# Hybrid decoder layer on one core: normalised x laid out at 2,304 bytes a part, input products cut at 256 columns, five offset places for split weights

## The chip, the core and the metric

The kernel runs on one core of one Trainium2 chip. The metric is device time in microseconds (us), from one launch of the program, lower is better. Five engines work side by side: PE (TensorE, matmuls; PEld is its weight load), DVE (VectorE), ACT (ScalarE), POOL (GpSimd) and SP (which here only issues DMAs). Each has its own in-order queue and waits for others by semaphores.

## What is computed

One decoder layer over 512 tokens of width 2,048 with 16 meta tokens put in front (528 columns in all), everything in float32:

```
n = rmsnorm(h) * g_mix;  p = n @ w_in           # 2048 x 6144
q, k, v, b, c, u = split(p, 6)                  # 1024 columns each
q, k = per-head rmsnorm (8 heads x 128)
z = q k^T / sqrt(128);  causal: key < query
w = exp(log_sigmoid(z) + reverse cumulative sum of log_sigmoid(-z))
o_attn = w v
o_conv = b * causal_conv3(c * u)
h = h + concat(rmsnorm(o_attn), rmsnorm(o_conv)) @ w_out
h = h + (silu(n2 @ w_gate) * (n2 @ w_up)) @ w_down;  n2 = rmsnorm(h)
return h without the meta columns
```

## The kernel before

All activations lie transposed: 128 channels on the partitions, tokens along the columns. Columns 0 to 15 are the meta tokens.

*Split products.* Matmuls run in the type float32r. To keep float32 accuracy each operand is split into a high part (the value cast to float32r) and a low part (value minus high part), and a product is the sum of three matmuls: high weights by high x (L168), high weights by low x (L170), low weights by high x (L172). ACT makes the high part by a cast, DVE the low part by a subtraction. Every matmul loads its 128 x 128 weights anew.

*Stage 1, start.* x arrives in 16 tiles xt (L233, SP's queue); split_x scales each by g_mix and makes nh and nl, two tiles of 528 columns (2,112 bytes a partition) for each of the 16; square_x gathers the squares for the norm. As the x tiles come in, the k and q products of head 0 run, FIRST giving the steps.

*Stage 1, weights.* prepare() loads weights into two places raw of eight 128-column tiles (512 KB a DMA, L132, SP), and splits four tiles at a time into whi (L136, ACT) and wlo (L137, DVE), each tag with five places; next_w keeps four sets ahead of the one in use. A set of a tag takes 2,048 bytes.

*Stage 1, products.* For each head k, q and v: k and v need all 528 columns, q needs 512. A PSUM bank holds 512 columns, so k and v go to two banks, 264 columns each. product_steps runs through the 16 x tiles, for each of them the matmuls of L168, L170 and L172 over all parts. Then qk_norm squares and copies the product out of PSUM (ACT), and after some tiles of the next product its finish normalises it (L328) and splits it for the attention; attend, sums and mix run in between the next products' matmuls, each released after a counted number of tiles by after and tick. After the eight heads come c, u and b for each of the eight channel groups: c and u in two halves of 258 columns (from column 12 on, since the convolution looks back two columns from column 16), b in 512.

*The rest.* The output projection (L670 to L672, weights w_out) and the feed-forward part (L684 to L686, a seven-product scheme in blocks of 256 columns) have their own pools of weights and activations. Their activations begin 16 bytes into a tile.

The steps of the prediction touch prepare (L126), product_steps (L161), split_x (L235), qk_norm (L302), head (L336), attend (L364) and the loop over c, u, b (L505 on), and the order of SP's DMA issues L132 and L233 at the start. The pieces that set the sizes:

```
H = L // 2
nh = npool.tile([P, L], F32R, tag=f"nh{k}", name=f"nh{k}")
product([(pv[:, 0, :H], 0, H), (pv[:, 1, :H], H, L)], n_hl)
C0, CH = 12, (L - 12) // 2
product([(pc[:, 0, :CH], C0, C0 + CH), (pc[:, 1, :CH], C0 + CH, L)], n_hl)
```

Of the kernel before, what the change touches and what calls it, by code (L numbers as in the profile page):

```python
# [9 lines left out]
F32 = mybir.dt.float32  # L10
# [5 lines left out]
P = 128  # L16
# [16 lines left out]
def hybrid_layer(ctx: ExitStack, tc: tile.TileContext, xT, w_in, w_out, w_gu, w_down, vecs, out):  # L33
# [47 lines left out]
        pe.matmul(warm[:, :P], ones, ones, start=True, stop=True)  # L81
    ident = const.tile([P, P], F32, name="ident")
    make_identity(nc, ident)
    later = const.tile([P, P], F32, name="later")
    gp.affine_select(
        out=later, in_=ones, pattern=[[-1, P]], compare_op=ALU.is_gt, fill=0.0, base=0,
        channel_multiplier=1,
# [31 lines left out]
                plan_w(w_in[c, b], 8)  # L119
    for b in range(2):  # L120
        plan_w(w_out[OUT_TILES[0], b], 8)
    raws, ready, taken = [], [], [0]
    SUB, AHEAD = 4, 4
    subs = [(i, a, min(a + SUB, n)) for i, (_, n) in enumerate(stream) for a in range(0, n, SUB)]

    def prepare():  # L126
        i, a, b = subs[len(ready)]
        with tc.high_priority():
            if i == len(raws):
                raws.append(wpool.tile([P, 8 * P], F32, tag="raw", bufs=2, name=f"raw{i}"))  # L130
                src, n = stream[i]
                nc.sync.dma_start(raws[i][:, : n * P], src)  # L132
            raw, c = raws[i][:, a * P : b * P], (b - a) * P
            hi = wpool.tile([P, SUB * P], F32R, tag="whi", bufs=AHEAD + 1, name=f"whi{i}_{a}")
            lo = wpool.tile([P, SUB * P], F32R, tag="wlo", bufs=AHEAD + 1, name=f"wlo{i}_{a}")
            sc.copy(hi[:, :c], raw)  # L136
            ve.tensor_tensor(lo[:, :c], raw, hi[:, :c].bitcast(F32), ALU.subtract)  # L137
        ready.append((hi, lo, b - a))
# [22 lines left out]
    def product_steps(parts, acts, n):  # L161

        k, last = 0, n - 1
        while k <= last:
            for wh, wl in next_w():
                ah, al = acts[k]
                for ps, a, b in parts:
                    pe.matmul(ps, wh, ah[:, a:b], start=k == 0, stop=False)  # L168
                for ps, a, b in parts:
                    pe.matmul(ps, wh, al[:, a:b], start=False, stop=False)  # L170
                for ps, a, b in parts:
                    pe.matmul(ps, wl, ah[:, a:b], start=False, stop=k == last)  # L172
                k += 1
                tick()
            yield
# [33 lines left out]

    H = L // 2  # L210
    n_hl = []
    accs = [rpool.tile([P, L], F32, name=f"acc_x{i}") for i in range(2)]

    acc = accs[0]
# [18 lines left out]
        nc.sync.dma_start(xts[k], xT[k])  # L233

    def split_x(k):  # L235
        nh = npool.tile([P, L], F32R, tag=f"nh{k}", name=f"nh{k}")
        nl = npool.tile([P, L], F32R, tag=f"nl{k}", name=f"nl{k}")
        g = g_mix[:, k : k + 1]
        if k < 4 or k % 2 == 0:
            sc.activation(nh, xts[k], AF.Copy, scale=g)  # L240
        else:
            gp.tensor_scalar(nh, xts[k], g, 0.0, ALU.mult, ALU.add)
        ve.scalar_tensor_tensor(nl, xts[k], g, nh.bitcast(F32), ALU.mult, ALU.subtract)
        n_hl.append((nh, nl))

    def square_x(k):
        if k < 2:
            sc.activation(accs[k], xts[k], AF.Square)
        else:
            s = t512(L, "r", 3)  # L250
            sc.activation(s, xts[k], AF.Square)
            (gp, ve)[k % 2].tensor_tensor(accs[k % 2], accs[k % 2], s, ALU.add)

    pk0 = pp.tile([P, 2, 512], F32, tag="pp", name="pk0")
    pq0 = pp.tile([P, 2, 512], F32, tag="pp", name="pq0")
    steps = [
        product_steps([(pk0[:, 0, :H], 0, H), (pk0[:, 1, :H], H, L)], n_hl, KT),
        product_steps([(pq0[:, 0, :], META, L)], n_hl, KT),
    ]
    prepare()  # L260
# [17 lines left out]


    apool = open_pool("apool", side="right")  # L280
    kns = [apool.tile([P, 640], F32, name=f"kn{i}") for i in range(1)]
    for t in kns:
        gp.memset(t[:, L:640], 0.0)
    oapool.tile([P, 8], F32, name="pad_oa")
    acc_c = oapool.tile([P, SEQ], F32, name="acc_c")
    acc_a = oapool.tile([P, SEQ], F32, name="acc_a")
# [6 lines left out]
    oa_all = o_slots(oapool, "oa", 4)  # L293
    oa = []

    def halves(ps, n):
        return ps[:, :, :n]

    def two(t):
        return t.rearrange("p (a b) -> p a b", a=2)  # L300

    def qk_norm(ps, g, cols, dst, parts_of, name):  # L302

        raw = t512(L, "e", 2)[:, :cols]
        s = t512(L, "e2", 2)[:, :cols]
        sh = apool.tile([P, L], F32R, tag="sh", name=f"sh_{name}")[:, :cols]
        sl = apool.tile([P, L], F32R, tag="sl", name=f"sl_{name}")[:, :cols]  # L310
        cuts = [(0, cols)] if cols == SEQ else [(0, H), (H, L)]
        raw_v, s_v = (raw, s) if cols == SEQ else (two(raw), two(s))
        sc.activation(s_v, ps, AF.Square)
        sc.activation(raw_v, ps, AF.Copy, scale=g)
        split(sh, sl, s)

        def finish():
            v = t512(L, "v", 2)[:, :cols]
            for a, b in cuts:
                q = small(f"ss_{name}{a}")[:, : b - a]  # L320
                pe.matmul(q, ones_r, sh[:, a:b], start=True, stop=False)
                pe.matmul(q, ones_r, sl[:, a:b], start=False, stop=True)
                ve.scalar_tensor_tensor(
                    v[:, a:b], q, 1.0 / P, eps_r2[:, L - cols + a : L - cols + b], ALU.mult, ALU.add
                )
            y = t512(L, "e2", 2)[:, :cols]
            rsqrt(y, v, cols)
            ve.tensor_tensor(dst, raw, y, ALU.mult)  # L328
            hi, lo, n = parts_of
            split(hi, lo, dst[:, :n])  # L330

        return finish

# [2 lines left out]
    def head(h):  # L336

        if h:
            pk = pp.tile([P, 2, 512], F32, tag="pp", name=f"pk{h}")
            product([(pk[:, 0, :H], 0, H), (pk[:, 1, :H], H, L)], n_hl)  # L340
        else:
            pk = pk0
        kn = kns[0]
        kh = apool.tile([P, 384], F32R, tag="kh", name=f"kh{h}")
        kl = apool.tile([P, 384], F32R, tag="kl", name=f"kl{h}")
        after(8, qk_norm(halves(pk, H), g_k, L, kn[:, :L], (kh, kl, 384), f"k{h}"))
# [6 lines left out]
        qn = apool.tile([P, SEQ], F32, tag="qn", name=f"qn{h}")  # L353
        qh = apool.tile([P, SEQ], F32R, tag="qh", name=f"qh{h}")
        ql = apool.tile([P, SEQ], F32R, tag="ql", name=f"ql{h}")
        after(9 if h else 10, qk_norm(pq[:, 0, :], gq_s, SEQ, qn, (qh, ql, SEQ), f"q{h}"))

        pv = pp.tile([P, 2, 512], F32, tag="pp", name=f"pv{h}")
        product([(pv[:, 0, :H], 0, H), (pv[:, 1, :H], H, L)], n_hl)
        vt = t512(L, "e", 2)  # L360
        ve.tensor_tensor(two(vt[:, :L]), halves(pv, H), two(r), ALU.mult)
        after(6 if h else 11, lambda: attend(h, kn, kh, kl, qn, qh, ql, vt))

    def attend(h, kn, kh, kl, qn, qh, ql, vt):  # L364
# [23 lines left out]
        pe.matmul(z[:, 272:416], kn[:, 384:512], qn[:, 368:], start=True, stop=True)  # L388
        pe.matmul(z[:, 416:432], kn[:, 512:640], qn[:, 496:], start=True, stop=True)


        lw = apool.tile([P, 1344], F32, tag="lw", name=f"lw{h}")
# [112 lines left out]
    C0, CH = 12, (L - 12) // 2  # L505
    oc = []
    for j in range(HEADS):
        pc = pp.tile([P, 2, 512], F32, tag="pp", name=f"pc{j}")
        product([(pc[:, 0, :CH], C0, C0 + CH), (pc[:, 1, :CH], C0 + CH, L)], n_hl)
        cu = t512(2 * CH, "e", 2)[:, : 2 * CH]  # L510
        ve.tensor_tensor(two(cu), halves(pc, CH), two(r2[:, C0:]), ALU.mult)
        pu = pp.tile([P, 2, 512], F32, tag="pp", name=f"pu{j}")
        product([(pu[:, 0, :CH], C0, C0 + CH), (pu[:, 1, :CH], C0 + CH, L)], n_hl)
        ve.tensor_tensor(two(cu), halves(pu, CH), two(cu), ALU.mult)
# [504 lines left out]
```

## Time and profile before

| | |
|---|---|
| three runs | 2108.03, 2109.98, 2113.12 us; median 2109.98 |
| profiled execution | 2107.92 us, of which the span from first to last instruction 2106.2 us |
| granted TensorE clock, mean | 0.998 of full speed |
| busy PE / DVE / ACT / POOL | 98 / 78 / 48 / 22% of the span |
| start, to the first pv matmul | 0 to 40.5 us |
| input products and attention | 40.5 to 627.5 us |
| output projection | about 627 to 775 us |
| feed-forward part | about 775 us to the end |

The page gives for each engine the busy time; a window row gives the same for a stretch of the execution. A row of the view in order of time reads: start, duration, engine, line, operation, out<-in, size, and in brackets what its engine waited for. Matmuls overlap in the pipeline, so what one costs is read from start to start. A row of a group reads: line, engine, operation, tiles, size, count, busy time and mean duration in ns of one, and then the idle time before them.

### The profile page before, as it was taken

What the parts mean: (1) busy time and instruction counts of PE and PEld (TensorE: products, weight loads), DVE (VectorE), ACT (ScalarE), POOL (GpSimd) and SP (SyncE); (2) the same over time, 40 slices, a digit from 0 to 9 for tenths busy, and PEclk for the clock granted to TensorE, in tenths of its full rate; (3) what the DMA queues carried; (4) which work ended last, traced back from release to release, by engine and by line L of the source; (5) the groups of instructions that cost most, each with busy time, mean ns of one, the idle gap of its engine ahead of it and who ended that gap; (6) DMA issues with size and microseconds to landing.
All of it is one profiled execution on the core that took longest, in us unless ns stands there. A gap on an engine that the chain in (4) does not pass through costs nothing.

```text
span 2106.2 us, 39382 instructions
## 1 busy us (share of the span) xinstructions
PE 2070.5 (98%) x16086; PEld 1987.5 (94%) x16086; DVE 1644.0 (78%) x2131; ACT 1019.5 (48%) x1576; POOL 458.9 (22%) x584
## 2 busy tenths in 40 slices
PE   8999999999999999999999999999999899999999
PEld 7999999999998888999999999999999899999999
DVE  8777767433337669999999998999989777877798
ACT  6666666322224344555555554555555444444443
POOL 4111111010003544122121221221111323122232
PEclk9999999999999999999999999999999999999999
DMA  5222222222235556566565565565554999788863
GB/s 173 81 72 80 74 78 81 81 97 94 91 110 172 177 181 221 166 184 179 172 190 166 154 193 165 172 178 160 170 153 146 304 280 278 202 232 246 241 190 121
DMA packets 146006, 342.48 MB, mean 163 GB/s; under 512 B 13393, under 2 KB 58961, under 8 KB 145825
## 3 DMA queue, kind: packets, MB, share of 16 engines
q1 hardware_dynamic: 67824, 214.33, 32.1%
q0 software_dynamic: 78000, 125.63, 21.9%
q8 instruction: 126, 2.06, 0.4%
q14 instruction: 56, 0.45, 0.1%
HBM read 268.60 MB, written 71.30 MB: 161 GB/s over the span
## 4 chain that ended last, share of the span: by engine, by line
PE 87%; DVE 5%; DMA 4%; issue 2%; ACT 1%; POOL 0%; SPq 0%; DVEq 0%; ACTq 0%
PE x L684 10%; PE x L686 9%; PE x L685 9%; PE z L684 5%; PE z L685 5%; PE z L686 5%; PE y L686 3%; PE y L685 3%; PE y L684 3%; PE po L671 3%; PE po L670 3%; PE po L672 3%; DMA b<-w_down 2%; DVE s L600 2%; PE pv L168 2%
## 5 line engine op out<-in xcount | busy, mean ns | idle before, releaser
L599 ACT CAST s<-t 128x1024 fp32r<-128x1024 f32 (+2 forms) x304 | 286.3, 942 | 395.3 <-PE z L686 127.6
L600 DVE TENSOR_TENSOR s<-t,s 128x1024 fp32r<-128x1024 f32 (+2 forms) x304 | 343.4, 1129 | 94.0 <-ACT s L599 92.5
L686 PE MATMUL x<-f,s 128*128 128x256 f32 x1408 | 387.3, 275 | 1.5 <-DVE s L600 1.5
L685 PE MATMUL x<-f,s 128*128 128x256 f32 x1408 | 387.4, 275 | 1.3 <-DVE f L183 1.3
L684 PE MATMUL x<-f,s 128*128 128x256 f32 x1408 | 387.3, 275 | 0.2 <-ACT f L182 0.2
L599 ACT CAST s<-b 128x1024 fp32r<-128x1024 f32 (+2 forms) x228 | 214.7, 942 | 221.7 <-PE x L686 202.1
L686 PEld LDWEIGHTS x<-f,s 128*128 128x128 f32 x1408 | 264.3, 188 | 1.7 <-DVE s L600 1.7
L685 PEld LDWEIGHTS x<-f,s 128*128 128x128 f32 x1408 | 264.3, 188 | 1.7 <-DVE f L183 1.5
L684 PEld LDWEIGHTS x<-f,s 128*128 128x128 f32 x1408 | 264.3, 188 | 0.5 <-ACT f L182 0.4
L600 DVE TENSOR_TENSOR s<-b,s 128x1024 fp32r<-128x1024 f32 (+2 forms) x228 | 248.1, 1088 | 3.1 <-ACT s L599 2.5
L137 DVE TENSOR_TENSOR wlo<-raw,whi 128x512 fp32r<-128x512 f32 (+1 forms) x198 | 142.3, 720 | 130.9 <-ACT whi L136 130.3
L868 POOL DMA_DIRECT2D fd<-s x154 | 108.8, 921 | 583.6 <-DVE s L183 582.1
L136 ACT CAST whi<-raw 128x512 fp32r<-128x512 f32 (+1 forms) x198 | 121.3, 614 | 185.3 <-PE pu L170 65.5
L684 PE MATMUL x<-ring,s 128*128 128x256 f32 x704 | 195.7, 278 | 8.6 <-DVE d L713 5.6
L684 PE MATMUL z<-f,s 128*128 128x256 f32 x704 | 195.8, 278 | 3.3 <-ACT p L705 3.1
L685 PE MATMUL x<-ring,s 128*128 128x256 f32 x704 | 194.8, 277 | 3.3 <-DMA ring<-fd 3.3
L686 PE MATMUL x<-ring,s 128*128 128x256 f32 x704 | 195.0, 277 | 0.4 <-DVE s L600 0.4
L686 PE MATMUL z<-f,s 128*128 128x256 f32 x704 | 193.9, 275 | 0.0
L685 PE MATMUL z<-f,s 128*128 128x256 f32 x704 | 193.9, 275 | 0.0
L606 DVE TENSOR_TENSOR t<-b,b 128x1024 f32<-128x1024 f32 (+2 forms) x152 | 166.4, 1094 | 27.8 <-DMA b<-w_down 23.2
L684 PEld LDWEIGHTS x<-ring,s 128*128 128x128 f32 x704 | 132.7, 189 | 10.7 <-issue 8.5
L684 PEld LDWEIGHTS z<-f,s 128*128 128x128 f32 x704 | 132.1, 188 | 6.5 <-ACT p L705 6.3
(326 smaller groups left out, 5599.0 us busy)
## 6 DMA issues: line engine op xcount, KB each, us to landing
b<-w_gu SPq DMA_DIRECT2D x176, 512.0 KB, 3.6
raw<-w_in SPq DMA_DIRECT2D x92, 512.0 KB, 3.3
fd<-s POOLq DMA_DIRECT2D x154, 256.0 KB, 5.3
b<-w_down SPq DMA_DIRECT2D x64, 384.0 KB, 3.9
ring<-fd POOLq DMA_DIRECT2D x28, 768.0 KB, 12.2
b<-w_down SPq DMA_DIRECT2D x64, 320.0 KB, 4.8
ring<-fd POOLq DMA_DIRECT2D x28, 640.0 KB, 11.3
wide<-w_out SPq DMA_DIRECT2D x30, 512.0 KB, 3.4
```

The lines of the kernel that those rows point to most:

```text
L136: sc.copy(hi[:, :c], raw)
L137: ve.tensor_tensor(lo[:, :c], raw, hi[:, :c].bitcast(F32), ALU.subtract)
L599: sc.copy(hi, src)
L600: ve.tensor_tensor(lo, src, hi.bitcast(F32), ALU.subtract)
L606: ve.tensor_tensor(sums[name], a, b, ALU.add)
L670: pe.matmul(ps, hi[:, kk], ah, start=k == 0, stop=False)
L671: pe.matmul(ps, hi[:, kk], al, start=False, stop=False)
L672: pe.matmul(ps, lo[:, kk], ah, start=False, stop=k == 7)
L684: pe.matmul(ps, hi[:, kk], act[:, 0, k], start=start and k == 0, stop=False, skip_group_check=not start)
L685: pe.matmul(ps, hi[:, kk], act[:, 1, k], start=False, stop=False, skip_group_check=not start)
L686: pe.matmul(ps, lo[:, kk], act[:, 0, k], start=False, stop=k == n - 1, skip_group_check=not start)
L868: gp.dma_start(fd[c][s][:, :, k], t[:, :, i])
```

## The change

- The normalised x is one tile n_all. Each of the 32 parts (high and low of 16 tiles) takes 576 columns, 2,304 bytes, which is nine times 256, and begins 4 columns in: all parts begin at the same residue modulo 256. In the layout of the program that is 240, the residue at which the feed-forward part's activations begin before and after.
- k, v, c and u go in parts of 256 and 272 columns: 256 into the second half of the first bank, 272 into the second bank, so that the 528 columns lie in one run in PSUM, and are read as one (across). c and u are now computed from column 0; the result is read from column 12 on as before.
- Split weights: high and low part lie in one tile w of 1,048 columns with five places. The part of it that is used begins at an offset that goes through 4, 0, 4, 8, 20 columns in turn. In the layout the five places begin at 16, 128, 48, 224 and 176 modulo 256; before, all began at 224.
- Raw weights: three places of four tiles, 256 KB a DMA, instead of two of eight.
- kn and qn keep only the columns that attend reads unsplit (144 of 528 and of 512; kn with its zeros is 256 wide), and the split parts are taken from the product in place; the mask "later" is a temporary.

On SP's queue the order of issues at the start becomes: three raw loads, xt 0 and 1, three raw loads, xt 2 to 4, three raw loads, xt 5 to 7, and so on; before: two raw loads, xt 0 to 2, two raw loads, xt 3 to 5, one raw load, xt 6, and so on.

```diff
-    later = const.tile([P, P], F32, name="later")
+    later = t512(P, "r", 3)
...
+    OFFSETS = (4, 0, 4, 8, 20)
...
-            if i == len(raws):
-                raws.append(wpool.tile([P, 8 * P], F32, tag="raw", bufs=2, name=f"raw{i}"))
-                src, n = stream[i]
-                nc.sync.dma_start(raws[i][:, : n * P], src)
-            raw, c = raws[i][:, a * P : b * P], (b - a) * P
-            hi = wpool.tile([P, SUB * P], F32R, tag="whi", bufs=AHEAD + 1, name=f"whi{i}_{a}")
-            lo = wpool.tile([P, SUB * P], F32R, tag="wlo", bufs=AHEAD + 1, name=f"wlo{i}_{a}")
+            c = (b - a) * P
+            raw = wpool.tile([P, SUB * P], F32, tag="raw", bufs=3, name=f"raw{i}_{a}")[:, :c]
+            nc.sync.dma_start(raw, stream[i][0][:, a * P : b * P])
+            at = OFFSETS[len(ready) % (AHEAD + 1)]
+            t = wpool.tile([P, 2 * SUB * P + 24], F32R, tag="w", bufs=AHEAD + 1, name=f"w{i}_{a}")
+            hi, lo = (t[:, at + h * SUB * P :][:, : SUB * P] for h in range(2))
...
+    LP = 576
+    n_all = npool.tile([P, 2 * KT * LP], F32R, name="n_all")
...
-        nh = npool.tile([P, L], F32R, tag=f"nh{k}", name=f"nh{k}")
-        nl = npool.tile([P, L], F32R, tag=f"nl{k}", name=f"nl{k}")
+        nh, nl = (n_all[:, a : a + L] for a in (4 + 2 * k * LP, 4 + (2 * k + 1) * LP))
...
+    def parts_of_two(ps, a, b):
+        return [(ps[:, 0, 512 - T2 :], a, a + T2), (ps[:, 1, : b - a - T2], a + T2, b)]
+
+    def across(ps, n):
+        return ps.rearrange("p a b -> p (a b)")[:, 512 - T2 : 512 - T2 + n]
...
-    kns = [apool.tile([P, 640], F32, name=f"kn{i}") for i in range(1)]
-    for t in kns:
-        gp.memset(t[:, L:640], 0.0)
+    kn = apool.tile([P, 256], F32, name="kn")
+    gp.memset(kn[:, L - 384 :], 0.0)
...
-        raw_v, s_v = (raw, s) if cols == SEQ else (two(raw), two(s))
-        sc.activation(s_v, ps, AF.Square)
-        sc.activation(raw_v, ps, AF.Copy, scale=g)
+        sc.activation(s, ps, AF.Square)
+        sc.activation(raw, ps, AF.Copy, scale=g)
...
-            ve.tensor_tensor(dst, raw, y, ALU.mult)
+            ve.tensor_tensor(dst, raw[:, late:], y[:, late:], ALU.mult)
             hi, lo, n = parts_of
-            split(hi, lo, dst[:, :n])
+            ve.tensor_tensor(raw[:, :n], raw[:, :n], y[:, :n], ALU.mult)
+            split(hi, lo, raw[:, :n])
...
-        product([(pv[:, 0, :H], 0, H), (pv[:, 1, :H], H, L)], n_hl)
+        product(parts_of_two(pv, 0, L), n_hl)
         vt = t512(L, "e", 2)
-        ve.tensor_tensor(two(vt[:, :L]), halves(pv, H), two(r), ALU.mult)
+        ve.tensor_tensor(vt[:, :L], across(pv, L), r, ALU.mult)
...
-        pe.matmul(z[:, 272:416], kn[:, 384:512], qn[:, 368:], start=True, stop=True)
-        pe.matmul(z[:, 416:432], kn[:, 512:640], qn[:, 496:], start=True, stop=True)
+        pe.matmul(z[:, 272:416], kn[:, :P], qn, start=True, stop=True)
+        pe.matmul(z[:, 416:432], kn[:, P:], qn[:, 128:], start=True, stop=True)
...
-        product([(pc[:, 0, :CH], C0, C0 + CH), (pc[:, 1, :CH], C0 + CH, L)], n_hl)
-        cu = t512(2 * CH, "e", 2)[:, : 2 * CH]
-        ve.tensor_tensor(two(cu), halves(pc, CH), two(r2[:, C0:]), ALU.mult)
+        product(parts_of_two(pc, 0, L), n_hl)
+        cu = t512(CN, "e", 2)[:, :CN]
+        ve.tensor_tensor(cu, across(pc, L)[:, C0:], r2[:, C0:], ALU.mult)
```

k's product (heads 0 to 7) and u's change as v's and c's do; the calls of qk_norm hand it the column from which the late part is kept, 384 for k and 368 for q.

More of the change, by code (lines that the diff above doesn't have):

```diff
@@ L121, in hybrid_layer @@
         plan_w(w_out[OUT_TILES[0], b], 8)
-    raws, ready, taken = [], [], [0]
+    ready, taken = [], [0]
+    OFFSETS = (4, 0, 4, 8, 20)
     SUB, AHEAD = 4, 4
@@ L256, in hybrid_layer @@
     steps = [
-        product_steps([(pk0[:, 0, :H], 0, H), (pk0[:, 1, :H], H, L)], n_hl, KT),
+        product_steps(parts_of_two(pk0, 0, L), n_hl, KT),
         product_steps([(pq0[:, 0, :], META, L)], n_hl, KT),
@@ L294, in hybrid_layer, with qk_norm @@
     oa = []
-    def halves(ps, n):
-        return ps[:, :, :n]
     def two(t):
         return t.rearrange("p (a b) -> p a b", a=2)
-    def qk_norm(ps, g, cols, dst, parts_of, name):
+    def qk_norm(ps, g, cols, late, dst, parts_of, name):
         raw = t512(L, "e", 2)[:, :cols]
@@ L339, in head @@
             pk = pp.tile([P, 2, 512], F32, tag="pp", name=f"pk{h}")
-            product([(pk[:, 0, :H], 0, H), (pk[:, 1, :H], H, L)], n_hl)
+            product(parts_of_two(pk, 0, L), n_hl)
         else:
             pk = pk0
-        kn = kns[0]
         kh = apool.tile([P, 384], F32R, tag="kh", name=f"kh{h}")
         kl = apool.tile([P, 384], F32R, tag="kl", name=f"kl{h}")
-        after(8, qk_norm(halves(pk, H), g_k, L, kn[:, :L], (kh, kl, 384), f"k{h}"))
+        after(8, qk_norm(across(pk, L), g_k, L, 384, kn[:, : L - 384], (kh, kl, 384), f"k{h}"))
         if h:
@@ L352, in head @@
             pq = pq0
-        qn = apool.tile([P, SEQ], F32, tag="qn", name=f"qn{h}")
+        qn = apool.tile([P, 144], F32, tag="qn", name=f"qn{h}")
         qh = apool.tile([P, SEQ], F32R, tag="qh", name=f"qh{h}")
         ql = apool.tile([P, SEQ], F32R, tag="ql", name=f"ql{h}")
-        after(9 if h else 10, qk_norm(pq[:, 0, :], gq_s, SEQ, qn, (qh, ql, SEQ), f"q{h}"))
+        after(9 if h else 10, qk_norm(pq[:, 0, :], gq_s, SEQ, 368, qn, (qh, ql, SEQ), f"q{h}"))
         pv = pp.tile([P, 2, 512], F32, tag="pp", name=f"pv{h}")
-        product([(pv[:, 0, :H], 0, H), (pv[:, 1, :H], H, L)], n_hl)
+        product(parts_of_two(pv, 0, L), n_hl)
         vt = t512(L, "e", 2)
-        ve.tensor_tensor(two(vt[:, :L]), halves(pv, H), two(r), ALU.mult)
+        ve.tensor_tensor(vt[:, :L], across(pv, L), r, ALU.mult)
         after(6 if h else 11, lambda: attend(h, kn, kh, kl, qn, qh, ql, vt))
@@ L503, in scale_a @@
         token_scale(acc_a, acc_a, 1024, "a", (sh, sl, t512(SEQ, "v", 2)[:, :SEQ], None, None))
-    C0, CH = 12, (L - 12) // 2
+    C0 = 12
+    CN = L - C0
     oc = []
@@ L508, in hybrid_layer @@
         pc = pp.tile([P, 2, 512], F32, tag="pp", name=f"pc{j}")
-        product([(pc[:, 0, :CH], C0, C0 + CH), (pc[:, 1, :CH], C0 + CH, L)], n_hl)
-        cu = t512(2 * CH, "e", 2)[:, : 2 * CH]
-        ve.tensor_tensor(two(cu), halves(pc, CH), two(r2[:, C0:]), ALU.mult)
+        product(parts_of_two(pc, 0, L), n_hl)
+        cu = t512(CN, "e", 2)[:, :CN]
+        ve.tensor_tensor(cu, across(pc, L)[:, C0:], r2[:, C0:], ALU.mult)
         pu = pp.tile([P, 2, 512], F32, tag="pp", name=f"pu{j}")
-        product([(pu[:, 0, :CH], C0, C0 + CH), (pu[:, 1, :CH], C0 + CH, L)], n_hl)
-        ve.tensor_tensor(two(cu), halves(pu, CH), two(cu), ALU.mult)
+        product(parts_of_two(pu, 0, L), n_hl)
+        ve.tensor_tensor(cu, across(pu, L)[:, C0:], cu, ALU.mult)
         y = t512(SEQ, "e2", 2)[:, :SEQ]
```

## The prediction

> **What bounds the kernel now.** I read the page first (busy shares, the chain of waits), then the stages by time window, then the instructions of TensorE in order of time, where the distance between two starts is the true price of a matmul; its own duration overlaps with the next one's and is of no use here.
>
> ```profile
> span 2106.2 us, 39382 instructions
> PE 2070.5 (98%) x16086; PEld 1987.5 (94%) x16086; DVE 1644.0 (78%) x2131; ACT 1019.5 (48%) x1576; POOL 458.9 (22%) x584
> PE 87%; DVE 5%; DMA 4%; issue 2%; ACT 1%; POOL 0%; SPq 0%; DVEq 0%; ACTq 0%
> 6.39:40.50 34.11, 28.95 (x148) 24.79 (x149) 32.94 (x39) 23.04 (x41) 20.70 (x14) 0.95 0.59 191
> 40.50:627.50 587.00, 585.97 (x4062) 549.47 (x4061) 351.30 (x604) 278.39 (x496) 68.19 (x126) 1.00 0.26 87
> ```
>
> The last two rows are windows: length, then busy time (and count) of PE, weight load, DVE, ACT and POOL, granted clock, DMA share, GB/s. The change touches two stages. From 6.39 to 40.5 us x arrives, is scaled and split, and heads 0 of k and q are multiplied; there VectorE is the full engine (32.94 of 34.11 us) and TensorE waits. From 40.5 to 627.5 us come all other input products and the attention; there TensorE is busy 585.97 of 587.00 us at clock 1.00, VectorE only 351. So in the second stage every nanosecond off a matmul is off the time; in the first none is.
>
> **What a matmul costs by its columns.** Starts in order of time (start, own duration, then the group):
>
> ```profile
> 1002.74 0.28 PE L686 MATMUL x<-f,s 128*128 128x256 f32 x1
> 1004.10 0.28 PE L686 MATMUL x<-f,s 128*128 128x256 f32 x1
> ...
> 207.07 0.40 PE L170 MATMUL pv<-nl,whi 128*128 128x264 f32 x2
> 209.72 0.40 PE L168 MATMUL pv<-nh,whi 128*128 128x264 f32 x2
> ...
> 479.14 0.40 PE L168 MATMUL pb<-nh,whi 128*128 128x512 f32 x1
> 490.24 0.40 PE L168 MATMUL pc<-nh,whi 128*128 128x258 f32 x2
> 501.81 0.40 PE L168 MATMUL pu<-nh,whi 128*128 128x258 f32 x2
> ...
> 768.04 0.39 PE L671 MATMUL po<-oc,s 128*128 128x512 f32 x1
> 769.40 0.39 PE L671 MATMUL po<-oc,s 128*128 128x512 f32 x1
> ```
>
> 256 columns: 12 matmuls in 1.36 us, 113.3 ns. 264 columns: 11 pairs in 2.65 us, 120.5 ns each. 258 columns: the whole product pc, 96 matmuls from 490.24 to 501.81, 120.5 ns each. 512 columns: 226.7 ns at best (6 in 1.36 us), 231.3 in pb (48 from 479.14 to 490.24). What the reader is to see: 258 and 264 cost the same, and 113.3, 120.5 and 226.7 are 16, 17 and 32 times 7.08 ns. The price goes by started groups of 16 columns, 7.08 ns each. Two halves of 264, or of 258, are 17 + 17 groups, 241.0 ns; 256 + 272 would be 16 + 17 groups, 233.7 ns. That is the core of the forecast.
>
> **The change part by part.** (a) *Parts of 256 and 272 for k, v, c, u.* A product is 16 tiles x 3 matmul pairs = 48 pairs:
>
> ```profile
> L168 PE MATMUL pv<-nh,whi 128*128 128x264 f32 x256 | 52.7, 287 | 0.0
> L168 PE MATMUL pc<-nh,whi 128*128 128x258 f32 x256 | 51.7, 284 | 0.0
> L168 PE MATMUL pb<-nh,whi 128*128 128x512 f32 x128 | 50.3, 393 | 0.0
> 144.07 0.28 PE L383 MATMUL z<-qh,kh 128*128 128x272 f32 x1
> 144.44 0.41 PE L388 MATMUL z<-qn,kn 128*128 128x144 f32 x2
> ```
>
> 256 rows of one kind over 8 heads are 16 pairs a product; three kinds make the 48. Without k's head 0, which lies in the first stage, 31 products remain in the saturated stage, 1488 pairs. At 233.7 for 241.0 ns that is 7.3 x 1488 = -10.9 us. Nothing here shows a 272 beside a 256. The nearest rows for 272 are the attention's three, 144.07 to 144.44: 123.3 ns each, 2.9 above 17 groups. With these the pair is 236.6 and the term -6.5 us. The other end is that both parts pay a group more than their number, as a part may that starts off its group: 247.9 ns, +10.3 us. I take -10.9, because the row with the same start (the x<-f rows of 256 columns begin, like all parts after the change, at 240 modulo 256 bytes in the layout) shows no excess in a thousand matmuls. That c and u now also multiply the 12 first columns, which nobody reads, is in the 233.7.
>
> (b) *Equal starts and the five places.* Before, the tiles of 2,112 bytes begin at four residues modulo 256; after, all parts begin at one, and the weights at five that depend on the place. For q and b (512 columns, 15 products x 48 = 720 matmuls in the stage) only this changes.
>
> ```profile
> 760.18 0.39 PE L670 MATMUL po<-oa,s 128*128 128x512 f32 x1
> 763.87 0.40 PE L671 MATMUL po<-oa,s 128*128 128x512 f32 x1
> 764.11 0.39 PE L672 MATMUL po<-oa,s 128*128 128x512 f32 x1
> 765.72 0.40 PE L670 MATMUL po<-oc,s 128*128 128x512 f32 x1
> ```
>
> Equal residues alone don't make 512 clean: oa has them too and averages 230.8 ns (24 in 5.54 us), a single one 240, while oc shows 226.7. From 231.3 the term lies between -3.3 us (226.7) and +6.3 us (240). I take 0: the nearest average, oa's, is where pb is already. The attention's operands also shift within their groups, some 35 matmuls a head; at half a group, 3.5 ns, that is +-1.0 us, taken as 0.
>
> (c) *Weights raw in three pieces of 4 tiles, not two of 8.* Twice as many DMA issues on SP.
>
> ```profile
> raw<-w_in SPq DMA_DIRECT2D x92, 512.0 KB, 3.3
> raw<-w_in SPq DMA_DIRECT2D x6, 256.0 KB, 2.8
>   DMA raw<-w_in: 3.5, 4
> ```
>
> A piece is reloaded when the piece three before has been split and is wanted three pieces later; four tiles are 12 pairs, 2.9 us, so it has 8.7 us for a landing of 2.8. The third row says what ACT waited for raw in the whole program: 3.5 us in 4 times. Nothing is behind these issues on SP in the saturated stage. Cost 0; without that cover every piece would be late by its landing less 2.9 us, which is below nothing.
>
> (d) *The start.* Here the moved issues count.
>
> ```profile
> 1.73 1.37 SPq L233 DMA_DIRECT2D xt<-xT  x3
> 5.49 0.81 SPq L132 DMA_DIRECT2D raw<-w_in  x2
> 6.34 1.37 SPq L233 DMA_DIRECT2D xt<-xT  x3
> 11.25 0.41 PE L168 MATMUL pk<-nh,whi 128*128 128x264 f32 x2
> 35.74 0.51 PE L170 MATMUL pk<-nl,whi 128*128 128x264 f32 x2 [1.43 <-DVE nl L243]
> ```
>
> SP issues x tiles 0 to 2 before its first wait now. After the change only tiles 0 and 1 stand there; tile 2 follows three raw loads, the last of which waits until VectorE has split the third piece, about 6.3 us by the start of the second raw pair here. So tile 2 is issued at about 6.7 instead of 3 us and lands near 10; on ACT its scaling stands behind the cast of the sixth piece, which waits for TensorE to be done with the first weights, near 10.7. TensorE wants tile 2 at 11.25 and gets it about 1 us late. The later x tiles move both ways, and VectorE, the full engine, has the same work in both. I take +1.0 us, between 0 (VectorE makes it up) and +3.
>
> (e) *The rest.* qk_norm multiplies the late 144 columns and the split columns apart: one more VectorE instruction.
>
> ```profile
> L328 DVE TENSOR_TENSOR kn<-tmp,tmp 128x528 f32<-128x528 f32 x8 | 5.6, 700 | 0.0
> L328 DVE TENSOR_TENSOR qn<-tmp,tmp 128x512 f32<-128x512 f32 x8 | 5.5, 686 | 0.1
> L183 DVE TENSOR_TENSOR kl<-kn,kh 128x384 fp32r<-128x384 f32 x8 | 4.4, 555 | 0.0
> 139.37 0.68 DVE L183 TENSOR_TENSOR ql<-qn,qh 128x512 fp32r<-128x512 f32 x1
> 143.07 0.39 PE L384 MATMUL z<-ql,kh 128*128 128x512 f32 x1
> ```
>
> By the slope from 384 to 528 columns (1.0 ns a column) 144 columns are 315 ns: k pays 315 + 555 - 700 = 170, q 315 ns, 0.49 us a head. ql is done at 140.05 and first used at 143.07: 3 us of cover, so 0; with no cover 8 x 0.49 = 3.9 us. Reading 516 or 528 columns in one run instead of two halves has the same count; the smaller kn, qn and the moved mask cost nothing.
>
> Sum: -10.9 + 0 + 0 + 1.0 + 0 = -9.9 us. The profiled execution took 2107.92 us (span 2106.2 and 1.7 around it), 0.1 below the lowest of the three runs and 2.1 below their median of 2109.98. From the profile the sum gives 2098.0, from the median 2100.1; I forecast 2099.0.
>
> **The rivals.** (1) *The 272 pays like the attention's*: the pair is 236.6, -6.5 + 1.0, 2103.5. For it: most matmuls in the trace whose columns are a whole number of groups lie above it (pb 231.3, oa 230.8). Against: x<-f. (2) *The excess eats the gain*: 256 and 272 have no slack inside their last group, where 258 and 264 hid misfits in 14 and 8 free columns; both pay half a group, 3.5 ns, the pair is 240.8, and the time 2109, no change. For it: pb and oa, half a group or more above 226.7. (3) *Slower: the price goes by columns, not by groups.* k and v keep their 528, c and u grow from 516 to 528 a pair; at (226.7 - 113.3) / 256 = 0.443 ns a column that is 5.3 ns x 768 pairs, +4.1, with the start 2114. It decides as soon as 258 is cheaper than 264; against it stand the rows, 120.5 for both. The Trainium skill has this rule: TensorE: Matmul & The Clock Gate, section Back-to-back issue gap, gives N / 2.4 + 2.5 ns on a warm clock, so 220.0 ns for 2 x 258 and 225.0 for 256 + 272, +3.8 us as an estimate from that page; the trace disagrees with it in level (113.3 where it has 109.2) and in the step from 258 to 264. (4) *Slower: both parts pay a whole group more*, since weights and x now meet in five fixed relations and a bad one repeats in every tile: 247.9 ns, +10.3 + 1.0, 2120. For it: 240 for a single oa matmul that recurs in each tile; against: x<-f and oc, with fixed relations and no excess.
>
> **How the numbers follow.** Forecast 0.55, rival 1 0.13, rival 2 0.11, rival 3 0.12, rival 4 0.09. 0.2%, some 4.2 us, is about what a measurement can tell from no change: faster is the forecast and rival 1, 0.68; the same is rival 2, 0.11; slower are rivals 3 and 4, 0.21. The likeliest case alone reaches from 2095 (512s clean as oc) to 2104 (start +3, attention +1). The range takes in rivals 1 to 3: 2093 to 2115; rival 4 is left out.
>
> **What would show it.** Right: in order of time, pairs of pv and pc 0.234 us apart, where 0.241 stands now; the window from the end of the start to the end of pb about 11 us shorter with TensorE still full; pb near 0.231; everything after it as long as before. Rival 1 shows 0.236 to 0.237, rival 2 0.241, rival 3 pc alone slower, rival 4 0.248. The start is wrong if the first pv begins before 40.5 or after 43.5 us. I'd be wrong altogether if TensorE begins to wait in the middle stage (for weights, or z for ql).

## The result: slower by 0.26%, and the profile after

The changed kernel took 2116.93 us in the median of ten runs (2112.93 to 2122.33), the kernel before 2113.12 us (2108.03 to 2119.12) beside it. The ratio is 1.0026, with a 95% interval of 1.0014 to 1.0039, some 3.0 to 8.2 us slower; the two medians by themselves lie 3.8 us apart. The forecast was 2099.0. The profiled execution took 2116.4 us, its span 2114.7 us, 8.5 more than before. That is more than the ratio gives: the profiled execution of before was faster than any of its ten runs.

The page of the changed kernel: the span, the busy times, the shares of the chain of waits, and the raw loads:

```profile
span 2114.7 us, 39641 instructions
PE 2076.6 (98%) x16086; PEld 1990.4 (94%) x16086; DVE 1652.8 (78%) x2147; ACT 1019.3 (48%) x1576; POOL 451.2 (21%) x584
PE 87%; DVE 6%; DMA 3%; issue 2%; ACT 2%; POOL 0%; SPq 0%; DVEq 0%; ACTq 0%; POOLq 0%
raw<-w_in SPq DMA_DIRECT2D x190, 256.0 KB, 2.8
```

Nothing new bounds it: TensorE is as full as before. So the windows are compared, cut at the same events in both kernels: the first matmul of head 0's v, of head 1's k, and of the last b, and for the third window the first matmul of x in the feed-forward part (columns as in the prediction's windows). Before:

```profile
6.39:40.52 34.13, 28.97 (x148) 24.81 (x149) 32.96 (x39) 23.06 (x41) 20.70 (x14) 0.95 0.59 191
54.54:616.15 561.61, 561.61 (x3911) 527.65 (x3909) 334.45 (x577) 268.10 (x479) 66.34 (x124) 1.00 0.26 83
807.05:2106.20 1299.15, 1271.38 (x11068) 1261.83 (x11066) 1133.82 (x1323) 644.32 (x924) 286.22 (x349) 1.00 0.67 195
```

After:

```profile
6.39:44.66 38.27, 30.90 (x149) 24.95 (x149) 33.26 (x40) 22.93 (x41) 17.91 (x14) 0.87 0.56 186
58.12:622.94 564.82, 564.67 (x3910) 529.47 (x3909) 343.79 (x593) 268.06 (x478) 61.47 (x124) 1.00 0.26 83
813.67:2114.70 1301.03, 1273.03 (x11068) 1263.04 (x11066) 1133.49 (x1323) 644.32 (x924) 286.05 (x349) 1.00 0.67 195
```

The reader is to see two places. The start is 4.1 us longer (38.27 for 34.13), though VectorE has the same work (33.26 and 32.96 us busy), and TensorE's granted clock is lower (0.87 for 0.95). The middle stage, where 11 us were to be gained, is 3.2 us longer (564.82 for 561.61), full in both, at full clock. The feed-forward part is 1.9 us longer, but that is not the change's: two executions of one kernel further down (two raw places) differ by 4.5 us in all that follows the middle stage, 1494.7 and 1490.2. The middle stage, however, repeats: 564.82 in both of these.

The price of a matmul in order of time, after:

```profile
485.37 0.39 PE L168 MATMUL pb<-n_all,w 128*128 128x512 f32 x1
496.51 0.41 PE L168 MATMUL pc<-n_all,w 128*128 128x256 f32 x2
508.14 0.40 PE L168 MATMUL pu<-n_all,w 128*128 128x256 f32 x2
```

The 48 pairs of pc take 11.63 us, 242.3 ns a pair, where 233.7 was forecast and 11.57 us, 241.0, stood before. The 48 matmuls of pb take 11.14 us, 232.1 ns, before 11.10.

Averaged over the stage, from the distances between starts in the two traces (ns; a pair is the sum of its two parts; the averages are good to some 0.2): before 120.7 for 258 and for 264 columns, pair 241.4, and 230.6 for 512 columns; after 117.0 for 256 and 125.6 for 272, pair 242.6, and 232.1 for 512. The stage of the windows holds 30 two-part products (1,440 pairs) and 14 of 512 columns (672 matmuls): +1.2 x 1440 + 1.5 x 672 ns = 2.7 of the 3.2 us. The 256 did save, 3.7 ns; the 272 cost 4.9.

### The profile page after: what moved, and what is told of

It reads as the page before. It is cut to its first block, busy times and chain, and to the rows that moved or that the text cites. A ratio compares the mean times of both kernels' runs of the same rounds, so it can differ in the third digit from the quotient of the medians.

```text
span 2114.7 us, 39641 instructions
## 1 busy us (share of the span) xinstructions
PE 2076.6 (98%) x16086; PEld 1990.4 (94%) x16086; DVE 1652.8 (78%) x2147; ACT 1019.3 (48%) x1576; POOL 451.2 (21%) x584
## 4 chain that ended last, share of the span: by engine, by line
PE 87%; DVE 6%; DMA 3%; issue 2%; ACT 2%; POOL 0%; SPq 0%; DVEq 0%; ACTq 0%; POOLq 0%
PE x L687 9%; PE x L689 9%; PE x L688 9%; PE z L687 5%; PE z L689 5%; PE z L688 5%; PE y L689 3%; PE y L688 3%; PE y L687 3%; PE po L674 3%; PE po L673 3%; PE po L675 3%; DMA b<-w_down 2%; DVE s L603 2%; PE pv L168 2%
## 5 line engine op out<-in xcount | busy, mean ns | idle before, releaser
L137 DVE TENSOR_TENSOR w<-raw,w 128x512 fp32r<-128x512 f32 (+1 forms) x198 | 141.3, 715 | 138.7 <-ACT w L136 137.5
L136 ACT CAST w<-raw 128x512 fp32r<-128x512 f32 (+1 forms) x198 | 121.5, 614 | 202.6 <-PE pu L172 66.5
```

## The experiments

Each is given as its edit of the changed kernel, if nothing else is said. Residues are start addresses modulo 256 bytes in the layout of the program; "x" is normalised x, "the stage" runs from head 1's first k matmul to the first matmul of the last b, as in the windows above. Where no ratio is given, the time is that of a single run; the kernel before alone spread over 11 us in ten runs, so such times decide little, and the stage and the matmul prices are read instead.

**Is it the alternation of banks?** Each tile's three matmuls of one part run before those of the other.

```diff
                 for ps, a, b in parts:
                     pe.matmul(ps, wh, ah[:, a:b], start=k == 0, stop=False)
-                for ps, a, b in parts:
                     pe.matmul(ps, wh, al[:, a:b], start=False, stop=False)
-                for ps, a, b in parts:
                     pe.matmul(ps, wl, ah[:, a:b], start=False, stop=k == last)
```

> Edit: in product_steps all three matmuls of one part run before the next part, so the PSUM bank changes twice a tile instead of six times; addresses as in the changed kernel. Theory A (an excess comes from changing the bank with every matmul): pairs near 234 ns, the stretch from the first pv to the last pb some 12 us shorter than the changed kernel's. Rival B (the excess comes from how the addresses of x and weights lie): pairs stay at 241 to 244 ns. Rival C (a fixed price of about 10 ns a matmul beside its columns): pairs stay at 240 to 243 ns. The start stays about 4 us late in all.

Measured: 118.0 and 124.8 ns, pair 242.8; stage 565.44; 2115.0 us. Theory A's 234 is missed: the order of the parts is not the cause. Between the rivals B and C this run doesn't decide.

**The five places.** All weights at 128, the residue of the feed-forward part's weights (the 24 spare columns go ahead of the pool).

```diff
-    OFFSETS = (4, 0, 4, 8, 20)
+    OFFSETS = (0, 0, 0, 0, 0)
```

> Edit: all five weight places at 128 modulo 256 (no offsets, 4,096 bytes a place), x at 240: the relation that the feed-forward part has. Theory B (addresses): the 256 part falls from 117 to 113.3 ns and the 272 part from 125.7 towards 120.4, pairs near 234. Rivals A and C: pairs stay at 241 to 244 ns. The start stays late.

Measured: 256 columns 114.7, 272 columns 125.7, 512 columns 233.1; stage 562.48; 2113.19 us. x at 240 and weights at 128 is the very relation of the x<-f rows, and here the 256 came near their 113.4, as theory B said. The 272 stayed where it was, so the pair, 240.4, is neither the theory's 234 nor quite the rivals' 241 to 244.

**The parts' sizes in the new layout.** 264 and 264 again, for all four products (and in `across` likewise).

```diff
-        return [(ps[:, 0, 512 - T2 :], a, a + T2), (ps[:, 1, : b - a - T2], a + T2, b)]
+        return [(ps[:, 0, 512 - H :], a, a + H), (ps[:, 1, : b - a - H], a + H, b)]
```

> Edit: parts of 264 and 264 again for k, v, c and u, all else as changed. If the price goes by started groups of 16 columns and 264 hides the misfits in its 8 free columns: 120.5 ns each, 241.0 a pair as before the change. If it is a fixed price of about 10 ns beside the columns: 120 ns each, 240 a pair. If equal residues are bad in themselves: over 242 a pair. c and u at 264 pay what k and v pay.

Measured: 122.3 ns each, pair 244.7; stage 567.96; 2122.67 us. The same 264 columns cost 120.7 in the layout before. In order of time:

```profile
498.77 0.40 PE L168 MATMUL pc<-n_all,w 128*128 128x264 f32 x2
510.57 0.41 PE L168 MATMUL pu<-n_all,w 128*128 128x264 f32 x2
```

11.80 us for a product, 245.8 ns a pair. That is over the 242 which the expectation gave for equal residues that are bad in themselves. So within the new layout the cut at 256 is worth 2 ns a pair, and the layout itself costs more than that.

**The start.** Two raw places of four tiles, not three.

```diff
-            raw = wpool.tile([P, SUB * P], F32, tag="raw", bufs=3, name=f"raw{i}_{a}")[:, :c]
+            raw = wpool.tile([P, SUB * P], F32, tag="raw", bufs=2, name=f"raw{i}_{a}")[:, :c]
```

> Edit: two raw places of four tiles instead of three, so that the issues of SP and the casts of ACT at the start stand in the order that they had before the change; all else as changed. If the order at the start is what costs: the first pv begins near 40.5 us instead of 44.7. If it is something else (matmul price, smaller pieces): it stays past 43. The middle stage stays as in the changed kernel, pairs near 243, unless two pieces are too few ahead: then ACT waits for raw.

Measured: first pv at 40.71 us (44.66 with three, 40.52 before), stage 564.82, 2115.56 us. So the order at the start is what cost there. Why three places were late shows in the changed kernel itself, first SP's queue, then ACT's:

```profile
0.82 1.34 SPq L132 DMA_DIRECT2D raw<-w_in  x3
2.20 0.91 SPq L235 DMA_DIRECT2D xt<-xT  x2
4.94 1.65 SPq L132 DMA_DIRECT2D raw<-w_in  x3
6.64 1.37 SPq L235 DMA_DIRECT2D xt<-xT  x3
9.14 3.25 SPq L132 DMA_DIRECT2D raw<-w_in  x3
12.45 1.38 SPq L235 DMA_DIRECT2D xt<-xT  x3
16.68 2.65 SPq L132 DMA_DIRECT2D raw<-w_in  x3
19.38 1.85 SPq L235 DMA_DIRECT2D xt<-xT  x4
...
30.50 0.91 SPq L235 DMA_DIRECT2D xt<-xT  x2
```

```profile
10.70 0.62 ACT L136 CAST w<-raw 128x512 fp32r<-128x512 f32 x1 [1.37 <-PE pk L172]
11.27 0.74 ACT L241 ACTIVATE n_all<-xt,vec 128x528 fp32r<-128x528 f32 x1
```

x tile 2 goes out at 6.64 and is scaled at 11.27, as forecast. But the pattern comes again with every three weights: the next x tiles wait behind raw loads that wait for a place, tile 8 until 19.38, and the last two until 30.50. Before, and with two places, the last x issue stands at 27.93 (the rows are those with two places; the first is x tiles 7 to 9):

```profile
10.55 1.38 SPq L235 DMA_DIRECT2D xt<-xT  x3
...
27.93 0.43 SPq L235 DMA_DIRECT2D xt<-xT  x1
```

The last issue is 2.6 us later. But that isn't the order's doing alone. The granted clock dropped where TensorE had been waiting; the windows from 16 to 29 us of the changed kernel (the last three numbers of a row are clock, DMA share and GB/s):

```profile
16.00:23.00 7.00, 4.07 (x23) 2.96 (x22) 6.34 (x7) 3.50 (x7) 5.05 (x4) 0.92 0.70 228
23.00:29.00 6.00, 6.00 (x22) 5.19 (x21) 4.99 (x6) 2.19 (x4) 2.77 (x3) 0.52 0.43 146
```

In 16 to 23 us TensorE had 4.07 us of work, in 23 to 29 it was full at a clock of 0.52. Another execution with the same start (three places; the experiment with the feed-forward weights, below) went without the drop, and its first pv stands at 42.50. Its window, and its issues of x tiles 8 to 11 and of the last two:

```profile
23.00:29.00 6.00, 5.16 (x27) 3.83 (x27) 5.89 (x7) 4.88 (x9) 5.08 (x4) 1.00 0.56 180
18.32 1.85 SPq L235 DMA_DIRECT2D xt<-xT  x4
28.11 0.90 SPq L235 DMA_DIRECT2D xt<-xT  x2
```

Without the drop the last issue is only 0.2 us later than with two places, but tiles 8 and 9 still go out at 18.32 and not from 10.55 on. So the delay in the middle of the queue costs some 2.0 us (42.50 for 40.52), and the slow clock the other 2.2 in the execution that was profiled. This split is rough: the one other execution with three places and no drop (part by part, above) has its first pv at 43.29, the four with a drop have it at 44.28 to 44.70, and the kernels with two places, the one before among them, have a drop of their own (clock 0.76 to 0.81 from 16 to 23 us). Over all profiles, three places gave a first pv at 42.50 to 44.70 us (six kernels, mean 44.0), two places of four tiles at 40.35 to 42.11 (five executions, mean 41.1).

**One residue for all.** Two raw places, x at 128 and weights at 128.

```diff
-        nh, nl = (n_all[:, a : a + L] for a in (4 + 2 * k * LP, 4 + (2 * k + 1) * LP))
+        nh, nl = (n_all[:, a : a + L] for a in (40 + 2 * k * LP, 40 + (2 * k + 1) * LP))
...
-    OFFSETS = (4, 0, 4, 8, 20)
+    OFFSETS = (0, 0, 0, 0, 0)
```

> Edit: parts of x begin at 128 modulo 256 (40 columns in, not 4), weights all at 128, two raw places; 256 and 272 as changed. This is the relation of the output projection's oc rows (226.7 ns). Theory B (the excess is set by the residues of x and weights, and the 272 part is dear because at 240 it starts 48 bytes into a 64-byte group and so touches 18 of them): at 128, a multiple of 64, the 272 part falls from 125.6 to 120.4, the 256 part to 113.3, pairs 234, middle stretch (first pk of head 1 to last pb) near 551 us. Rival D (a part of 272 costs 125 wherever it lies): pairs 239 to 240. Rival E (start on a 64-byte line is bad for 256): 256 above 117.

Measured: 256 columns 118.3 to 119.6 by product, 272 columns 125.0 to 127.7, 512 columns 229.9; stage 567.19, the worst but one; first pv at 40.65; 2120.83 us. A pair costs 244.6 to 246.0, so theory B's 234 is missed by more than 10, and a start on a multiple of 64 bytes makes neither part cheap. Of the rivals, E's price for the 256 held (above 117), and D's 125 for the 272 at best.

**The parts alone.** The kernel before, with its layout, raw pieces and weights, and only the parts of 256 and 272 columns.

```diff
-        product([(pv[:, 0, :H], 0, H), (pv[:, 1, :H], H, L)], n_hl)
+        product(parts_of_two(pv, 0, L), n_hl)
```

(and so for k, c and u, whose results are read across).

> Edit: the kernel before with parts of 256 and 272 for k, v, c and u and nothing else; x tiles of 2,112 bytes at four residues, weights all at 224, start as before. If the parts themselves lose (256 and 272 have no free columns in their last group): pairs at 242 to 243, middle stretch some 3 us longer than before, 564 to 565. If the equal residues and five places lose, and the parts win: pairs near 234 to 237, middle stretch 551 to 556.

Measured: 117.5 and 123.2 ns, pair 240.6, 512 columns 230.2; stage 560.19, 1.4 less than before; 2107.34 us. Neither branch of the expectation came (242 to 243, or 234 to 237): the parts alone win, but little. By starts of x the 256 ranged from 115.8 (160) to 118.2 (32), and 512 columns from 225.7 (224) to 232.1 (32).

**The row that the forecast rested on.** In the feed-forward part, where 256 columns cost 113.4 at x 240 and weights 128, x is moved to 224 (first diff), or the weights to 224 (second, by padding their pools).

```diff
-        t = t[:, 4 : 4 + c].rearrange("p (s a k t) -> p s a k t", s=m, a=2, k=n)
+        t = t[:, 0:c].rearrange("p (s a k t) -> p s a k t", s=m, a=2, k=n)
```

```diff
-    hpool.tile([P, 24], F32, name="pad_h")
...
-    pad(fpool, 160)
+    pad(fpool, 256)
...
-    pad(rings_p[1], 160)
+    pad(rings_p[1], 256)
```

> Edit: in the changed kernel the feed-forward activations begin at 224 modulo 256 instead of 240 (the 4 columns in front go behind), weights stay at 128. If the residue of x decides: its 256-column matmuls rise from 113.4 to 115 or more and the feed-forward part grows by some 20 us or more. If it doesn't: 113.4 and no growth.

> Edit: in the changed kernel the weights of the output projection and the feed-forward part begin at 224 modulo 256 instead of 128, activations stay at 240. If the residue of the weights decides: the 256-column matmuls rise from 113.4 to some 116.6 (what the place at 224 costs in the input products) and the feed-forward part grows by 30 us or more. If it doesn't: 113.4.

Measured: 2168.98 and 2150.85 us. The window from 1000 to 1100 us of the changed kernel, then of x at 224, then of weights at 224:

```profile
1000.00:1100.00 100.00, 99.42 (x871) 98.83 (x870) 91.13 (x99) 51.58 (x69) 18.56 (x24) 1.00 0.59 176
```

```profile
1000.00:1100.00 100.00, 100.00 (x836) 100.00 (x835) 87.25 (x94) 48.98 (x65) 20.89 (x26) 1.00 0.58 174
```

```profile
1000.00:1100.00 100.00, 100.00 (x845) 100.00 (x844) 87.52 (x96) 49.56 (x67) 18.26 (x24) 1.00 0.57 172
```

Matmuls of the same kind at the same clock, 871, 836 and 845 of them in 100 us. For the x<-f group the mean distance is 113.4, 120.0 and 117.7 ns, and the spans are 52.6 and 34.4 us longer than the changed kernel's. Both operands' starts count. The x at 224 shows an even 120.0:

```profile
1010.22 0.29 PE L687 MATMUL x<-f,s 128*128 128x256 f32 x1
...
1011.30 0.28 PE L687 MATMUL x<-f,s 128*128 128x256 f32 x1
```

Nine in 1.08 us. By the Trainium skill (TensorE: Matmul & The Clock Gate, section Back-to-back issue gap) the isolated gap is N / 2.4 + 2.5 ns, a rule in which no address appears; for 256 columns that is 109.2 ns, an estimate from the page. The trace disagrees: in this stream the three distances lie 4 to 11 ns above it, and they differ.

**Can the starts be chosen?** From the parts alone the best starts were read: x at 160 and weights at 224, so that q and b begin at 224. Two raw places.

```diff
-    OFFSETS = (4, 0, 4, 8, 20)
+    OFFSETS = (0, 0, 0, 0, 0)
...
+            t = wpool.tile([P, 2 * SUB * P], F32R, tag="w", bufs=AHEAD + 1, name=f"w{i}_{a}")
...
-        nh, nl = (n_all[:, a : a + L] for a in (4 + 2 * k * LP, 4 + (2 * k + 1) * LP))
+        nh, nl = (n_all[:, a : a + L] for a in (48 + 2 * k * LP, 48 + (2 * k + 1) * LP))
```

> The changed kernel with two raw places, all five weight places starting at 224 modulo 256 bytes (no offsets, 4,096 bytes a place) and every part of normalised x at 160, so that q and b start at 224; parts stay 256 and 272. Theory (the start addresses of x and of the weights set a product's pace, and what parts alone showed at these starts holds when all products have them): 256 columns at 115.8 and 272 at 122.1 ns, a pair at 237.9 against 241.0 before; 512 columns at 225.7 against 230.6; from the second head's k to the last b some 1,390 x 3.1 + 700 x 4.9 ns = 7.7 us less than before's 561.6, 553.9 us; the first pv at 40.4 to 40.8 us; the time some 8 us below before (ratio 0.996). Rival (the starts were only a label for a tile's place in the chain, and the mean of parts alone is the price): a pair at 240.6 and 512 columns at 230, the stage at 560, the time 1 to 2 us below before. Rival (equal starts of all parts cost by themselves, as in the changed kernel): a pair at 242.9, the stage at 564.8, the time 2 to 4 us above before.

And with halves of 264, which begin at 192 and 224 (weights and raw places as above):

```diff
-        nh, nl = (n_all[:, a : a + L] for a in (4 + 2 * k * LP, 4 + (2 * k + 1) * LP))
+        nh, nl = (n_all[:, a : a + L] for a in (2 * k * LP, (2 * k + 1) * LP))
...
-        return [(ps[:, 0, 512 - T2 :], a, a + T2), (ps[:, 1, : b - a - T2], a + T2, b)]
+        return [(ps[:, 0, 512 - H :], a, a + H), (ps[:, 1, : b - a - H], a + H, b)]
```

> The same with equal parts of 264 and 264 columns (258 and 258 are not restored: c and u take 264 as well), the weights at 224, the first half of x at 192 and the second at 224 modulo 256, q and b at 0. Theory of the starts: 264 columns at 119.0 (start 192) and 118.4 (start 224), a pair at 237.4; 512 columns at 0 were not seen, between 225.7 (start 224) and 232.1 (start 32); the stage from the second head's k to the last b between 553.2 and 557.6 us; the parts' sizes then decide little, and the time is 4 to 9 us below before. Rival (the mean of a tile's place is the price): a pair at 241.0 to 244.6 (as before and as the halves in the changed layout), the stage at 561 to 568, the time from 0 to 8 us above before.

Measured: x at 160 took 2107.12 us against 2110.01 beside it, ratio 0.9983 (0.9972 to 0.9994), faster than both kernels. Stage 558.77: 256 columns 115.9 as read, but 272 columns 124.2 (122.1 was read) and 512 columns 228.0 (225.7). With 264 halves: 2111.19 us, 1.0004 (0.9992 to 1.0016); 120.0 and 120.4 ns (119.0 and 118.4 read), 512 columns 233.1; stage 562.46. In order of time, x at 160:

```profile
477.49 0.40 PE L168 MATMUL pb<-n_all,w 128*128 128x512 f32 x1
488.37 0.41 PE L168 MATMUL pc<-n_all,w 128*128 128x256 f32 x2
499.90 0.40 PE L168 MATMUL pu<-n_all,w 128*128 128x256 f32 x2
```

The 48 matmuls of pb take 10.88 us, 226.7 ns each, and the 48 pairs of pc 11.53 us, 240.2. The stage lies nearest to the first rival's 560, below it; the theory's 553.9 was missed. A price read at one start of x, where neighbours start elsewhere, did not carry whole to a layout where all start there (why is not shown). The direction held, and the size only for 256. The first pv, at 41.63, missed its 40.4 to 40.8 too, with a clock of 0.65 in the 4.5 us before 40.5. With the halves of 264 the stage fell into the rival's 561 to 568.

**The two terms in the time.** The kernels with two raw places and with the parts alone once more, each timed over a dozen runs.

> The changed kernel with two raw places in place of three, timed in rounds. Theory (the changed kernel's loss is two terms: some 4 us at the start, from the third raw place, and some 3 us between the second head's k and the last b, from the starts of x and weights): the first is gone, the second stays, first pv at 40.5 to 40.9 us, the stage at 564.8, the ratio to before between 1.000 and 1.0018. Rival (the start gives nothing back in the end, something later catches it): the ratio stays at 1.0026.

> The kernel before with parts of 256 and 272 columns alone, timed in rounds. Theory (the cut alone is worth the 0.4 to 0.9 ns of a pair that one look showed): the stage from the second head's k to the last b at 560.2 against 561.6, the ratio 0.999 to 1.000. Rival (the prediction's term of 10.9 us, which the addresses alone took away): 0.995. Rival (the cut itself loses, 272 paying more than 256 saves): the stage above 562, the ratio above 1.0005.

Measured: 2113.28 against 2112.32 us, ratio 1.0008 (0.9996 to 1.0021), and 2110.18, 0.9991 (0.9982 to 1.0000). The stages are the earlier ones to the hundredth, 564.82 and 560.19. Both theories held in ratio and stage. The first pv with two places was at 42.11 this time, not at 40.5 to 40.9; the window before it is one of half clock again, first this execution, then the earlier one of the same kernel:

```profile
36.00:40.50 4.50, 4.50 (x19) 3.88 (x19) 3.81 (x7) 2.39 (x5) 0.00 (x0) 0.62 0.37 125
```

```profile
36.00:40.50 4.50, 4.50 (x25) 3.65 (x25) 3.83 (x7) 2.36 (x5) 0.00 (x0) 1.00 0.38 121
```

The loss and its parts fit together: 3.2 us in the stage and some 3 at the start (the 2.9 between the mean first pv of three and of two places) make 6 us, where the ratio gives 3.0 to 8.2. From three to two raw places the ratio falls by 0.0018, 3.8 us, but these two intervals overlap, so the times alone don't show this; the first pv does. The parts alone give 1.9 us in time (0.0009, with 1.0000 at the end of the interval), 1.4 in the stage.

## Why the prediction was wrong, point by point

Against the 2098.0 that the sum gives from the profile, the profiled execution is 18.4 us later: some 14 of them in the middle stage, 3.1 at the start, 1.9 in the feed-forward part, which the change does not touch, and 0.7 less in the stretches between.

*What bounds the kernel*: right. Every nanosecond off or on a matmul in the middle stage was on the time.

*(a) Parts of 256 and 272*: the step that failed. "The price goes by started groups of 16 columns, 7.08 ns each" was read off 113.3 for 256 and 120.5 for 258 and 264. The first number belongs to x at 240 with weights at 128, the others to parts that begin at eight places each, with weights at 224. Sorted by these places, the 258-column matmuls of the kernel before cost from 117.9 ns (start 208) to 123.5 (start 24) and the 264 from 118.4 (224) to 122.0 (0): that both came to 120.5 was an average over starts, not a price of 17 groups. "I take -10.9, because the row with the same start ... shows no excess in a thousand matmuls" matched x's start and not the weights'. With those at five places the 256 costs 117.0 instead of 113.4; with all at 128 it costs 114.7. And not even a matmul's own two starts fix its price: one of the five places is 128, and there the 256 of the changed kernel costs 116.5, no less than at the others (116.2 to 118.0). The larger miss is the 272: 125.6 where 17 groups are 120.4, at every place of the weights (125.2 to 126.0). The pair came to 242.6; the term is +1.8 us over 1,488 pairs where -10.9 was taken, within the bounds given, far from the value taken. The attention's 272 at 123.3, the nearest row with the right number of columns, was set aside for a row of other columns.

*(b) Equal starts, five places*: 0 was taken, +1.1 measured (1.5 ns x 720), within its bounds. The rows it went by, oa and oc, begin at 240 and 128; q and b leave out the 16 meta columns and so begin 64 bytes into a part, at 48. But these starts also moved the price of (a): the parts alone, in the old layout, gained 1.4 us in the stage; with the new layout the stage lost 3.2. That the starts do it, and not the rest of the change, is seen where only they differ: x at 160 and weights at 224 brought the stage from 564.82 to 558.77.

*(c) Three raw pieces in the saturated stage*: right, 0. With three places and with two the stage has the same 564.82 us.

*(d) The start*: the mechanism was right to the microsecond for x tile 2, its size was not: +1.0 was taken, +3 the bound, +4.1 measured at the first pv, of which 3.6 are left when head 1's k begins (58.12 for 54.54). The step followed the first round of the new order only. Each later round delays x again, and in most executions a slow clock, which the forecast didn't count, comes on top.

*(e) One more VectorE instruction*: right, 0; TensorE idles 0.15 us in the whole middle stage (564.67 busy of 564.82).

*The rivals.* The first's 123.3 for the 272 was seen in the parts alone (123.2), but its 113.3 for the 256 was not; and the reason given for it, that most matmuls with whole groups lie above their number, does not hold by count: the 256-column matmuls of the feed-forward part, over 11,000 of the 16,086, lie on it. The second (both parts pay half a group, 240.8) was nearest in kind: the excess ate the gain, though mainly by the 272. It forecast 2109 with +1.0 for the start; 1.8 ns more a pair, (b) and the start's other 3 us make the rest. The third, by columns, ended at 2114, near the time, for another reason: its price was to be seen in pc alone, but k and v pay as much (243.0 a pair, c and u 242.2). A whole group more each (247.9) was not seen.

*Still open*: by which rule the starts set the price. The order of the banks is excluded; that x's start and the weights' start each count is shown; the start of the matmul before, or of the weights that load meanwhile, may be the rest, which wasn't tried, nor was the start of the result in PSUM moved by itself.

## What to carry to other kernels

Take a matmul's price only from a row in which the columns and the starts of both operands are those of the new code; if one of them differs, that row is only a hint, and even with both the same it can miss by some 2 ns, as the 272 at x 160 did (122.1 read, 124.2 measured). Be wary of an average over several starts. Measure a layout on one stage before it is given to all; here x at 160 and weights at 224, together with two raw places, made of the slower kernel one that is 0.17% faster than before. When a load is given more buffers, write out the whole order of its queue to the end of the stage, not the first round, and see which other loads stand behind its waits.

## What the hardware showed beside that

The start address of an operand was worth up to 6% of a matmul here: 256 columns at 113.4, 117.7 or 120.0 ns with nothing else changed in the feed-forward part, and moving x there from 240 to 224 made the span 2167.3 us where the changed kernel's is 2114.7.

After waits of TensorE its matmuls ran at half rate for some microseconds, in some executions of a kernel and not in others. In the changed kernel's start, first a wait of 0.75 us, then 512 columns:

```profile
22.58 0.81 PE L170 MATMUL pk<-n_all,w 128*128 128x256 f32 x2 [0.75 <-DVE n_all L244]
...
25.37 0.63 PE L172 MATMUL pq<-n_all,w 128*128 128x512 f32 x1
25.80 0.63 PE L168 MATMUL pq<-n_all,w 128*128 128x512 f32 x1
26.23 0.63 PE L170 MATMUL pq<-n_all,w 128*128 128x512 f32 x1
```

0.43 us from start to start, against 0.23 later. The Trainium skill (TensorE: Matmul & The Clock Gate, section Back-to-back issue gap) gives N / 1.2 for a cold clock, 427 ns for 512 columns, and the trace agrees.
